# Attention scores of two heads: a zero-padded 128-row matmul, or two 64-row matmuls on separate halves of the array

## The chip, the cores and the metric

The kernel runs on one core of a Trainium2 chip. The metric is the device time of one execution in microseconds (us), from launch to end; smaller is better. A profile of one execution shows what each engine did: PE is the matrix engine (PEld are its weight loads, which the profile lists apart), DVE the vector engine, ACT the scalar engine, POOL the general one, SP the queue that issues most of the DMAs. In a matmul the first operand is *stationary* (it is loaded into the array ahead of time) and the second *moving* (it streams through, one column after the other); the result goes to PSUM, which has eight banks of 512 f32 columns per partition.

## The reference, cut to what matters

A four-layer decoder trunk with 256 tokens, model width 1024 and head width 64. Layers 0 and 3 use differential attention, layer 1 block-sparse attention (with 256 tokens it is plain causal attention), layer 2 grouped attention with a window of 128, a bias and sinks. Each layer is followed by a squared-ReLU MLP. What the change touches is the product of queries and keys, which in every layer is made for 16 head maps of width 64:

```python
# differential: H = 8 heads, each with two maps c (q and k are 64 wide)
s = jnp.einsum('bqhcd,bkhcd->bhcqk', qi, k)
s = jnp.where(causal, s, -inf); p = softmax(s)
p = p[:, :, 0] - lam * p[:, :, 1]
# block-sparse and windowed layers: 16 heads of width 64
s = einsum('...qd,...kd->...qk', q, k)
```

## The kernel before, in words

All products are done on f32 values split into a high and a low part. A value x is copied to the type f32r (the high part), and x minus that copy is the low part. A product then takes three matmuls: high by high, high by low, low by high (`mm3`, L269 to L273). Where the high and low parts of the moving operand lie side by side, two instructions do (`block_step`, L571 to L573).

Weights come in pieces of 1 MB by DMA (`fetch`). `stage` splits each piece with four ACT copies (L79, tile `whi`) and four DVE subtractions (L80, tile `wlo`); `take` keeps this two pieces ahead of the matmuls. The instructions are emitted in the order of the Python code, and a list scheduler then orders each engine's queue; semaphores are placed by it. It may move independent matmuls of a projection (`p_in`) in between those of the attention.

A mixer layer (`mixer_layer`) makes its projections one after the other. In layers 0, 1 and 3 the order is v, pair 0, pair 1, v, pair 2, pair 3, where a *pair* c brings the queries and keys of four heads (two *blocks* of two heads). Layer 2 has one key block for all, and four pieces of queries. While one projection runs, the blocks of the pair before it are worked off: the first in the middle of it (`midway`), the second after it. So there are 8 blocks in a layer and 32 in all. After the last projection nothing of the kind is left to run beside the last two blocks except the output projection (`out_proj`, tile `p_d`), which needs the blocks' results one after the other.

A block goes through `turn` (queries and keys are transposed by PE into a PSUM bank, tile `p_qk`), `put_q` (L467 and L468, tile `qhl`), `put_k` (L471 to L475, keys into the tiles `kpadh` and `kpadl`), `scores` (L311), the softmax (L331 on DVE, L334 on ACT), a transposition (`p_t`, L349), the product with v (`p_av`), and a transposition back (`p_o`, L374) into `oo`.

The two heads of a block lie on partitions 0 to 63 and 64 to 127 of one transposed query tile. So that one matmul over all 128 rows gives the scores of both heads side by side, the keys are stored padded: `kpad` has a place for each head of the two, and the 64 partitions of the other head hold zeros there. `new_keys` (L359) makes the zeros with eight POOL memsets (L365) at each layer, and `put_k` writes only the 64 partitions that belong to the head, in one ACT copy and one DVE subtraction for each head:

```python
for h in range(2):
    s = slice(HD * h, HD * h + HD)
    A.activation(k[0][s, :n, h, :], p[s], AF.Copy)
    V.tensor_tensor(k[1][s, :n, h, :], p[s], f(k[0][s, :n, h, :]), op=OP.subtract)
```

A block's scores are then six matmuls with 128 rows: for the first 128 tokens three with 2 x 128 = 256 moving columns into bank `p_s0`, for the other 128 tokens three with 2 x 256 = 512 columns into bank `p_s1` (both are called `p_s` in the profile).

Of the kernel before, what the change touches and what calls it, by code (L numbers as in the profile page):

```python
# [24 lines left out]
HD = 64  # L25
# [9 lines left out]
def f(ap):  # L35
    return ap.bitcast(F32)
# [3 lines left out]
def trunk(ctx: ExitStack, tc: tile.TileContext, xT, positions, gains, lams, swa_row, fng, weights, out):  # L40
    nc = tc.nc
    V, A, G, T = nc.vector, nc.scalar, nc.gpsimd, nc.tensor
# [226 lines left out]
    def mm3(out, lh, ll, rh, rl, start, stop, **kw):  # L269

        T.matmul(out, lh, rh, start=start, stop=False, **kw)  # L271
        T.matmul(out, lh, rl, start=False, stop=False, **kw)  # L272
        T.matmul(out, ll, rh, start=False, stop=stop, **kw)  # L273
# [37 lines left out]
    def scores(q, k, mask, sinks):  # L311


        p0, p1 = bank("wk", "p_s0"), bank("wk", "p_s1")
        (qh, ql), (kh, kl) = q, k
        for p, t, n in ((p0, 0, P), (p1, 1, S)):
            o = p[:, :2 * n].rearrange("p (h m) -> p h m", h=2)
            a = slice(P * t, P * t + P)
            mm3(o, qh[:, a], ql[:, a], kh[:, :, :n], kl[:, :, :n], True, True)
        out = []  # L320
        scored[0] += 1
        pair_e = room(4 + scored[0] % 2, [P, 2, 3 * P], "e")
        for c in range(2):
            ns = sb.tile([P, 3 * P], F32, tag="ns", name="ns", bufs=2)
            nm = tiny.tile([P, NT], F32, tag="nm", name="nm", bufs=4)
            l = tiny.tile([P, NT], F32, tag="l", name="l", bufs=6)
            e = pair_e[:, c]
            mk = mask[:, :, :].rearrange("p a b -> p (a b)")
            for t, p, n in ((0, p0, P), (1, p1, S)):
                s = slice(0, P) if t == 0 else slice(P, 3 * P)  # L330
                V.tensor_tensor_reduce(ns[:, s], p[:, n * c:n * c + n], mk[:, s], op0=OP.add, op1=OP.min,  # L331
                                       scale=-1.0, scalar=3.0e38 if sinks is None else sinks[c][1],
                                       accum_out=nm[:, t:t + 1])
# [24 lines left out]

    def new_keys():  # L359

        kpad = [[room(10 + 2 * j + x, [P, 2, 2, S], f"kpad{'hl'[x]}{j}", F32R) for x in range(2)] for j in range(2)]
        for j in range(2):
            for x in range(2):
                for h in range(2):
                    G.memset(f(kpad[j][x][HD * (1 - h):HD * (1 - h) + HD, :, h, :]), 0.0)  # L365
        return kpad

    pair = []

# [82 lines left out]
    def turn(src, n):  # L452

        p = bank("wk", "p_qk")
        for b in range(n):
            for t in range(NT):
                at = S * b + P * t
                T.transpose(p[:, at:at + P], src(b, t), ident)
        return p[:, :S * n].rearrange("p (b m) -> p b m", m=S)
# [9 lines left out]
        return q  # L469

    def put_k(k, p, n):  # L471
        for h in range(2):
            s = slice(HD * h, HD * h + HD)
            A.activation(k[0][s, :n, h, :], p[s], AF.Copy)
            V.tensor_tensor(k[1][s, :n, h, :], p[s], f(k[0][s, :n, h, :]), op=OP.subtract)  # L475

    def mixer_layer(i, n):
        mixer, slot = i % 3, i // 3
        r = norm_factor(n)
        parts = []  # L480
        kpad = new_keys()
        if mixer == 2:
            bias = room(8, [P, 1024], "bias")
            rest = room(9, [P, 1024], "rest")
# [4 lines left out]
            p = proj(n, (256, 1), True)  # L489
            kv = rest[:, 512:1024].rearrange("p (t c) -> p t c", t=NT)  # L490
            for t in range(NT):
                V.scalar_tensor_tensor(kv[:, t, :], p[t], r[:, t:t + 1], rest[:, :256],
                                       op0=OP.mult, op1=OP.add)
            rope(kv[:, :, 0:P].rearrange("p t (s e) -> p t s e", e=HD), 2)
            put_k(kpad[0], turn(lambda b, t: kv[:, t, 0:P], 1), 1)
            kT = [x[:, 0] for x in kpad[0]]
            first, second = [], []
            for c in range(4):
                p = proj(n, (256, 1), False, first)
                qn = room(c % 2, [P, NT, 256], "qn")  # L500
                for t in range(NT):
                    for h in range(2):
                        s = slice(P * h, P * h + P)
                        o = qn[:, t, :].rearrange("p (b h e) -> p b h e", h=2, e=HD)[:, :, h, :]
# [6 lines left out]
                qs = []  # L511
# [12 lines left out]
        else:  # L524
            v = [room(8 + j, [P, NT, 512], f"v{j}") for j in range(2)]
            vdone = 0
            first, second = [], []
            for c in ("v", 0, 1, "v", 2, 3):
                p = proj(n, (512, 2), vdone == 0, first)
                if i == 0 and used[0] == 2:  # L530
                    rotary_tables()
                    lambdas()
                if c == "v":
                    for t in range(NT):
                        A.activation(v[vdone][:, t, :], p[t], AF.Copy, scale=r[:, t:t + 1])
# [12 lines left out]

                def block(b, c=c, qs=qs, qk=qk):
                    if b == 0:  # L550
                        qs += put_q(turn(lambda j, t: qk[:, t, P * j:P * j + P], 2))
                        put_k(kpad[c % 2], turn(lambda j, t: qk[:, t, P * (2 + j):P * (2 + j) + P], 2), 2)
                    q, k = [x[:, b] for x in qs], [x[:, b] for x in kpad[c % 2]]
                    h = 2 * c + b
                    vh = lambda m: v[h // 4][:, m, P * (h % 4):P * (h % 4) + P]
                    if mixer == 0:
                        step(diff_block(parts, slot, q, k, vh, h))
                    else:
                        step(head_block(parts, q, k, vh, causal, None, h))

                first, second = [lambda f=block: f(0)], [lambda f=block: f(1)]
# [228 lines left out]
```

## Time and profile before

| | |
|---|---|
| median of three runs | 1183.45 us (1182.74 to 1184.18) |
| the profiled execution | 1184.6 us, of which its instructions span 1182.8 us |
| mean granted clock of TensorE | 0.994 |
| PE, PEld, DVE, ACT, POOL busy | 1154.8, 993.3, 860.0, 705.9, 19.7 us |

How to read the rows. In the groups, a row is: line, engine, operation, written tile <- read tiles, shape written <- shape read, times it ran | busy us in all, mean ns of one | idle us of the engine just before them and what ended that idle time. In the timeline, a row is: start in us, duration in us, engine, line, operation and tiles, and, in brackets, the idle time before it and what ended it; x8 means that eight of them are merged into the row. In the stages, a row is: start:end, length, busy us of each engine with its instructions, granted clock, DMA share and GB/s. The end of a matmul is modelled: its duration holds time in which the next is already streaming, so what matmuls cost in a row is read from the distance of their starts.

### The profile page before, as it was taken

Reading aid. Unit: us, or ns where it says so; the run is one execution under the profiler, and the core shown is the slowest. Engines: PE = TensorE matmul, PEld = TensorE weight load, DVE = VectorE, ACT = ScalarE, POOL = GpSimd, SP = SyncE. Lnnn points to the kernel's source line nnn. Section 1 sums busy time; section 2 is a strip of 40 time slices with the busy share of each in tenths; the row PEclk is TensorE's granted clock in tenths of the full one; section 3 lists DMA queues with packets and bytes.
Section 4 is the critical chain, followed back from the end, with each engine's and each line's share of the span. In section 5 each row is a group of like instructions: output and inputs, shape, how many; then the busy total and the mean of one; then the engine's idle time right before and its main releaser. Section 6 shows DMA issues by size and latency. Waiting matters only on the chain.

```text
span 1182.8 us, 17907 instructions
## 1 busy us (share of the span) xinstructions
PE 1154.8 (98%) x6448; PEld 993.3 (84%) x6448; DVE 860.0 (73%) x2190; ACT 705.9 (60%) x1619; POOL 19.7 (2%) x55
## 2 busy tenths in 40 slices
PE   9997999999999999999999999999999989999996
PEld 7885888888888888888899988888888868888885
DVE  6989988656665698775668798775557798777453
ACT  7786766555466775554547775654447776566341
POOL 2000000000100000000010000000010000000000
PEclk9999999999999999999999999999999999999999
DMA  8532455555544255555563245555654433555541
GB/s 323 199 132 104 143 201 191 182 209 179 180 160 157 73 178 178 184 208 178 183 224 111 75 153 206 190 202 178 201 189 144 143 107 108 186 182 178 188 174 37
DMA packets 30122, 198.74 MB, mean 168 GB/s; under 512 B 3536, under 2 KB 4688, under 8 KB 6608
## 3 DMA queue, kind: packets, MB, share of 16 engines
q1 hardware_dynamic: 29744, 197.06, 48.4%
q8 instruction: 51, 0.84, 0.3%
q10 hardware_dynamic: 288, 0.52, 0.1%
q14 instruction: 39, 0.32, 0.1%
HBM read 196.52 MB, written 1.05 MB: 167 GB/s over the span
## 4 chain that ended last, share of the span: by engine, by line
PE 93%; DVE 4%; ACT 2%; DMA 0%; issue 0%; SPq 0%
PE p_up L572 20%; PE p_down L572 15%; PE p_up L573 10%; PE p_down L573 8%; PE p_in L272 6%; PE p_in L273 6%; PE p_in L271 6%; PE p_e L572 3%; PE p_d L572 2%; PE p_last L273 2%; PE p_last L272 2%; PE p_last L271 2%; PE p_t L349 1%; PE p_e L573 1%; DVE wlo L80 1%; PE p_d L573 1%
## 5 line engine op out<-in xcount | busy, mean ns | idle before, releaser
L80 DVE TENSOR_TENSOR wlo<-raw,whi 128x512 fp32r<-128x512 f32 x740 | 484.2, 685 | 239.9 <-ACT whi L79 239.3
L79 ACT ACTIVATE whi<-raw 128x512 fp32r<-128x512 f32 x740 | 419.9, 623 | 295.2 <-PE p_up L572 106.7
L572 PE MATMUL p_up<-hg,whi 128*128 128x512 f32 x1024 | 358.3, 395 | 0.0
L573 PE MATMUL p_up<-hg,wlo 128*128 128x256 f32 x1024 | 285.2, 279 | 0.0
L572 PE MATMUL p_down<-uu,whi 128*128 128x512 f32 x768 | 266.4, 393 | 0.0
L572 PEld LDWEIGHTS p_up<-hg,whi 128*128 128x128 f32 x1024 | 192.0, 188 | 44.5 <-DVE hg L229 0.2
L573 PE MATMUL p_down<-uu,wlo 128*128 128x256 f32 x768 | 213.5, 278 | 0.0
L573 PEld LDWEIGHTS p_up<-hg,wlo 128*128 128x128 f32 x1024 | 192.9, 188 | 0.2
L572 PEld LDWEIGHTS p_down<-uu,whi 128*128 128x128 f32 x768 | 143.9, 187 | 32.8
L573 PEld LDWEIGHTS p_down<-uu,wlo 128*128 128x128 f32 x768 | 144.5, 188 | 0.0
L271 PE MATMUL p_in<-whi,hg 128*128 128x512 f32 (+1 forms) x368 | 137.1, 374 | 0.1
L272 PE MATMUL p_in<-wlo,hg 128*128 128x512 f32 (+1 forms) x368 | 136.0, 370 | 0.2 <-DVE wlo L80 0.2
L273 PE MATMUL p_in<-whi,hg 128*128 128x512 f32 (+1 forms) x368 | 135.6, 368 | 0.0
L272 PEld LDWEIGHTS p_in<-wlo,hg 128*128 128x128 f32 x368 | 69.6, 189 | 12.4 <-DVE wlo L80 1.5
L271 PEld LDWEIGHTS p_in<-whi,hg 128*128 128x128 f32 x368 | 69.5, 189 | 11.6 <-ACT whi L79 0.7
L273 PEld LDWEIGHTS p_in<-whi,hg 128*128 128x128 f32 x368 | 69.5, 189 | 10.7
L578 ACT ACTIVATE cross<-p_up 128x256 f32<-128x256 f32 x128 | 48.1, 376 | 31.2 <-ACT whi L79 22.3
L334 ACT ACTIVATE e<-ns,nm 128x256 f32<-128x256 f32 (+1 forms) x128 | 56.7, 446 | 14.4 <-DVE nm L331 14.0
L572 PE MATMUL p_d<-oo,whi 128*128 128x512 f32 x128 | 50.9, 428 | 10.2 <-DVE oo L384 10.2
L579 DVE TENSOR_TENSOR relu<-p_up,cross 128x256 f32<-128x256 f32 x128 | 53.2, 417 | 0.3
L271 PE MATMUL p_last<-whi,uu 128*128 128x512 f32 x128 | 49.8, 389 | 0.0
L273 PE MATMUL p_last<-whi,uu 128*128 128x512 f32 x128 | 49.8, 389 | 0.0
(182 smaller groups left out, 1368.9 us busy)
## 6 DMA issues: line engine op xcount, KB each, us to landing
raw<-in_weights SPq DMA_DIRECT2D x183, 1024.0 KB, 4.9
raw<-in_weights SPq DMA_DIRECT2D x8, 256.0 KB, 5.7
hT<-in_xT SPq DMA_DIRECT2D x4, 256.0 KB, 5.8
bias<-in_swa_row SPq DMA_DIRECT2D x1, 512.0 KB, 5.2
grow<-in_fng SPq DMA_DIRECT2D x1, 512.0 KB, 3.7
out<-res ACTq DMA_DIRECT2D x2, 256.0 KB, 2.8
out<-res SPq DMA_DIRECT2D x2, 256.0 KB, 2.7
lv<-in_lams SPq DMA_DIRECT2D x1, 256.0 KB, 6.4
```

The source lines that it names most:

```text
L79: A.activation(hi[:, s], raw[:, s], AF.Copy)
L80: V.tensor_tensor(lo[:, s], raw[:, s], f(hi[:, s]), op=OP.subtract)
L271: T.matmul(out, lh, rh, start=start, stop=False, **kw)
L272: T.matmul(out, lh, rl, start=False, stop=False, **kw)
L273: T.matmul(out, ll, rh, start=False, stop=stop, **kw)
L334: A.activation(e[:, s], ns[:, s], AF.Exp, bias=nm[:, t:t + 1], scale=-1.0, accum_out=l[:, t:t + 1])
L349: T.transpose(p[:, P * j:P * j + P], e[:, P * j:P * j + P], ident)
L572: T.matmul(r3(2)(p), hi, x, start=start, stop=False, skip_group_check=True)
L573: T.matmul(p[:, :S], lo, x[:, 0], start=False, stop=stop, skip_group_check=True)
L578: A.activation(cross, p[:, S:], AF.Copy)
L579: V.tensor_tensor(out, p[:, :S], cross, op=OP.add)
```

## The change

The keys are no longer padded. A tile `kk` holds for a pair the high and low part of both blocks' keys, with head 0 on partitions 0 to 63 and head 1 on partitions 64 to 127, as the transposition left them. `new_keys` no longer sets zeros, and `put_k` is one ACT copy and one DVE subtraction over 128 partitions.

`scores` now issues, for each of the two token halves and each of the three products, one matmul for each head: rows 0 to 63 for head 0, rows 64 to 127 for head 1, each into a bank of its own (`ps_h[0]`, `ps_h[1]`). That is 12 matmuls with 64 rows instead of six with 128, with 128 and 256 moving columns instead of 256 and 512. A head's bank holds both token halves, so the softmax's reads (L331) of a head come from one bank instead of two.

```diff
-        p0, p1 = bank("wk", "p_s0"), bank("wk", "p_s1")
+        ps_h = [bank("wk", f"p_s{c}") for c in range(2)]
         (qh, ql), (kh, kl) = q, k
-        for p, t, n in ((p0, 0, P), (p1, 1, S)):
-            o = p[:, :2 * n].rearrange("p (h m) -> p h m", h=2)
+        for cols, t, n in ((slice(0, P), 0, P), (slice(P, 3 * P), 1, S)):
             a = slice(P * t, P * t + P)
-            mm3(o, qh[:, a], ql[:, a], kh[:, :, :n], kl[:, :, :n], True, True)
+            for x, y, first, last in ((qh, kh, True, False), (qh, kl, False, False), (ql, kh, False, True)):
+                for c in range(2):
+                    r = slice(HD * c, HD * c + HD)
+                    T.matmul(ps_h[c][:, cols], x[r, a], y[r, :n], start=first, stop=last)
...
-            for t, p, n in ((0, p0, P), (1, p1, S)):
+            for t in range(NT):
                 s = slice(0, P) if t == 0 else slice(P, 3 * P)
-                V.tensor_tensor_reduce(ns[:, s], p[:, n * c:n * c + n], mk[:, s], op0=OP.add, op1=OP.min,
+                V.tensor_tensor_reduce(ns[:, s], ps_h[c][:, s], mk[:, s], op0=OP.add, op1=OP.min,
...
     def new_keys():
-        kpad = [[room(10 + 2 * j + x, [P, 2, 2, S], f"kpad{'hl'[x]}{j}", F32R) for x in range(2)] for j in range(2)]
-        for j in range(2):
-            for x in range(2):
-                for h in range(2):
-                    G.memset(f(kpad[j][x][HD * (1 - h):HD * (1 - h) + HD, :, h, :]), 0.0)
-        return kpad
+        return [room(10 + j, [P, 2, 2, S], f"kk{j}", F32R) for j in range(2)]
...
     def put_k(k, p, n):
-        for h in range(2):
-            s = slice(HD * h, HD * h + HD)
-            A.activation(k[0][s, :n, h, :], p[s], AF.Copy)
-            V.tensor_tensor(k[1][s, :n, h, :], p[s], f(k[0][s, :n, h, :]), op=OP.subtract)
+        A.activation(k[:, 0, :n], p, AF.Copy)
+        V.tensor_tensor(k[:, 1, :n], p, f(k[:, 0, :n]), op=OP.subtract)
...
-                    q, k = [x[:, b] for x in qs], [x[:, b] for x in kpad[c % 2]]
+                    q, k = [x[:, b] for x in qs], [kk[c % 2][:, x, b] for x in range(2)]
```

More of the change, by code (lines that the diff above doesn't have):

```diff
@@ L480, in mixer_layer @@
         parts = []
-        kpad = new_keys()
+        kk = new_keys()
         if mixer == 2:
@@ L494, in mixer_layer @@
             rope(kv[:, :, 0:P].rearrange("p t (s e) -> p t s e", e=HD), 2)
-            put_k(kpad[0], turn(lambda b, t: kv[:, t, 0:P], 1), 1)
-            kT = [x[:, 0] for x in kpad[0]]
+            put_k(kk[0], turn(lambda b, t: kv[:, t, 0:P], 1), 1)
+            kT = [kk[0][:, x, 0] for x in range(2)]
             first, second = [], []
@@ L551, in block @@
                         qs += put_q(turn(lambda j, t: qk[:, t, P * j:P * j + P], 2))
-                        put_k(kpad[c % 2], turn(lambda j, t: qk[:, t, P * (2 + j):P * (2 + j) + P], 2), 2)
-                    q, k = [x[:, b] for x in qs], [x[:, b] for x in kpad[c % 2]]
+                        put_k(kk[c % 2], turn(lambda j, t: qk[:, t, P * (2 + j):P * (2 + j) + P], 2), 2)
+                    q, k = [x[:, b] for x in qs], [kk[c % 2][:, x, b] for x in range(2)]
                     h = 2 * c + b
```

## The prediction

> **What bounds the kernel now.** I read the page first, for the busy shares and the chain that ended last.
>
> ```profile
> PE 1154.8 (98%) x6448; PEld 993.3 (84%) x6448; DVE 860.0 (73%) x2190; ACT 705.9 (60%) x1619; POOL 19.7 (2%) x55
> ...
> PE 93%; DVE 4%; ACT 2%; DMA 0%; issue 0%; SPq 0%
> ```
>
> PE holds 93% of the chain. So a change to its work counts almost in full, and work taken from DVE, ACT or POOL counts only where PE waits for it. There are as many weight loads as matmuls (6448 each): every matmul brings its own load. Second, the stages, to see where PE does wait:
>
> ```profile
> 14.00:92.00 78.00, 77.69 (x388) 63.35 (x387) 68.81 (x262) 61.85 (x153) 0.00 (x0) 1.00 0.58 212
> 92.00:119.00 27.00, 18.69 (x109) 14.46 (x108) 23.48 (x124) 16.55 (x58) 0.00 (x0) 1.00 0.22 79
> ...
> 948.00:980.00 32.00, 25.54 (x131) 20.14 (x129) 27.70 (x151) 20.22 (x70) 0.00 (x0) 0.84 0.29 99
> ```
>
> While projections run (14 to 92 us here) PE is busy without a hole. In the last two blocks of layers 0 and 3 (92 to 119, 948 to 980) it is not: there PE idles 8.3 and 6.5 us, and the chain of each block through DVE and ACT sets the pace. I call these four blocks the tails; the other 28 run under a full PE. Third, the groups of the scores, each shape by itself:
>
> ```profile
> L271 PE MATMUL p_s<-kpadh,qhl 128*128 128x512 f32 x32 | 13.7, 428 | 0.0
> ...
> L273 PE MATMUL p_s<-kpadh,qhl 128*128 128x256 f32 x32 | 9.1, 284 | 0.0
> ```
>
> First and last of six such rows, one for each product and shape: 32 blocks of six matmuls. Their durations overlap, so fourth, the timeline of one block under a full PE, for the distance of their starts:
>
> ```profile
> 53.28 0.28 PE L273 MATMUL p_s<-kpadh,qhl 128*128 128x256 f32 x1
> 53.28 0.19 PEld L271 LDWEIGHTS p_s<-kpadh,qhl 128*128 128x128 f32 x1
> ...
> 53.40 0.39 PE L271 MATMUL p_s<-kpadh,qhl 128*128 128x512 f32 x1
> 53.40 0.19 PEld L272 LDWEIGHTS p_s<-kpadl,qhl 128*128 128x128 f32 x1
> 53.63 0.40 PE L272 MATMUL p_s<-kpadl,qhl 128*128 128x512 f32 x1
> ...
> 54.09 1.03 PE L458 MATMUL p_qk<-ident,qk 128*128 128x128 f32 x8
> ```
>
> A matmul with 256 columns costs 53.40 - 53.28 = 0.12 us, one with 512 costs 53.63 - 53.40 = 0.23. The load of a matmul starts when the matmul before it starts, so it is hidden. A block costs 3 x 0.12 + 3 x 0.23 = 1.05 us, all 32 cost 34 us: that is all there is to win here, 3% of the span, and half of it is the most that two heads side by side can give.
>
> **The matmuls.** After the change each head has its own: 6 with 128 columns and 6 with 256. The nearest row for 128 columns is the last one above, eight transpositions of 128 x 128: (1.03 - 0.27) / 7 = 0.11 us each, where 0.27 is the duration of one of them. They are not of this type, but each also needs a load, and the loads above follow each other at 0.12; so I take 0.11.
>
> If the two heads' matmuls run side by side, loads included, a pair costs what one costs: 3 x 0.11 + 3 x 0.12 = 0.69 us, 0.36 less than now. If they take turns, all 12 count: 6 x 0.11 + 6 x 0.12 = 1.38, which is 0.33 more. No matmul in this trace uses less than 128 rows, so both ends stand. I take the first: adjacent matmuls of the new code differ in rows, stationary operand and bank, so they share nothing that the code shows. For the 28 blocks under a full PE that is 28 x 0.36 = 10.1 us less.
>
> The Trainium skill, "TensorE: Matmul & The Clock Gate", part "Packing small matmuls", says of matmuls on different row groups that they run concurrently, with starts some 4 ns apart; by that rule a block is at 0.69. No run here shows it yet, and the section "LDWEIGHTS" adds that a load's time goes by its columns and not its rows, so that 64-row loads would be no cheaper; if they also queue, a block is at 1.38.
>
> **The switch of shape.** The array goes from 128 rows to 64 at each block and back: 64 switches. Their price is not in this trace. The lower end is nothing: around the block above PE goes over to transpositions (54.09) after two steps of 0.23 after 53.63, with one more score between and no gap. The upper end is a pipeline that has to run empty with the load behind it. A matmul's duration goes beyond its share by 0.28 - 0.12 = 0.16, and what a load costs when it is not hidden is in the tail of layer 0:
>
> ```profile
> 95.32 0.38 PE L349 MATMUL p_t<-ident,e 128*128 128x128 f32 x2
> 96.90 0.62 PE L271 MATMUL p_s<-kpadh,qhl 128*128 128x256 f32 x2 [1.20 <-ACT kpadh L474]
> 97.63 0.39 PE L272 MATMUL p_s<-kpadl,qhl 128*128 128x256 f32 x1
> 97.85 0.28 PE L273 MATMUL p_s<-kpadh,qhl 128*128 128x256 f32 x1
> 97.97 0.40 PE L272 MATMUL p_s<-kpadl,qhl 128*128 128x512 f32 x1
> ```
>
> The matmul at 97.63 has waited for its operand, so its load is bare: the next starts 0.22 later, where the next pair is 0.12 apart. A bare load costs 0.10 to 0.11. So a switch costs 0 to 0.16 + 0.11 = 0.27 us. I take 0.11, a bare load, between the ends and the nearest thing that PE shows when its flow is broken: 64 x 0.11 = 7.0 us more.
>
> **The keys.** `put_k` runs 13 times, and in each one ACT copy and one DVE subtraction go, while the others grow from 64 to 128 partitions. Growing costs nothing: `put_q`'s copy on 128 partitions takes the 587 ns of `put_k`'s on 64.
>
> ```profile
> L475 DVE TENSOR_TENSOR kpadl<-p_qk,kpadh 64x512 fp32r<-64x512 f32 x24 | 16.4, 684 | 5.7 <-ACT kpadh L474 5.6
> ...
> L474 ACT ACTIVATE kpadh<-p_qk 64x512 fp32r<-64x512 f32 x24 | 14.1, 587 | 3.7 <-DVE kpadl L475 3.5
> ...
> L467 ACT ACTIVATE qhl<-p_qk 128x512 fp32r<-128x512 f32 x16 | 9.4, 587 | 3.1 <-PE p_qk L458 3.1
> ```
>
> DVE and ACT are relieved of about half of 16.4 and 14.1 us, POOL of most of the 19.7 us it is busy in all. Under a full PE this is worth nothing: at 14 to 92 us DVE has 9 us to spare, and if the six blocks there make that stretch 2.2 us shorter, DVE's own work shrinks by three subtractions, 2.1 us. The cover holds.
>
> In the tail it counts. The row of L474 names an order that the code does not ask for: ACT's copy for head 1 waits for DVE's subtraction for head 0. In time:
>
> ```profile
> 93.12 0.58 ACT L474 ACTIVATE kpadh<-p_qk 64x512 fp32r<-64x512 f32 x1
> ...
> 96.25 0.59 ACT L474 ACTIVATE kpadh<-p_qk 64x512 fp32r<-64x512 f32 x1
> 95.19 0.67 DVE L475 TENSOR_TENSOR kpadl<-p_qk,kpadh 64x512 fp32r<-64x512 f32 x1
> ...
> 96.88 0.69 DVE L475 TENSOR_TENSOR kpadl<-p_qk,kpadh 64x512 fp32r<-64x512 f32 x1 [0.20 <-ACT kpadh L474]
> 956.80 0.60 ACT kpadh L474
> ```
>
> The first score starts at 96.90 (the fence above), when the second copy ends. After the change the high keys are whole at 93.7 and the low ones, with DVE's queue unchanged, at 95.9. The transpositions ahead of the scores on PE (95.32, two of them at 0.11) leave it at about 95.5, so the scores start 1.4 us earlier, and their second part at 95.9 instead of 97.63. The last row, from the chain of waits, has the same step in layer 3. What comes next is DVE's softmax, which in the tails is 87% busy (23.48 of 27), so the gain may shrink to nothing; I take 1.4 for each tail, 2.8 us less.
>
> **The later read.** A head's bank now holds both token halves. If the order is kept by bank, the first read of head 0 waits for 11 of 12 matmuls instead of three of six.
>
> ```profile
> 102.67 0.36 PE L271 MATMUL p_s<-kpadh,qhl 128*128 128x256 f32 x1
> 103.31 0.29 DVE L331 CUSTOM_DVE_ANT_0 ns<-p_s,causal 128x128 f32<-128x128 f32 x1
> ...
> 104.65 0.42 DVE L331 CUSTOM_DVE_ANT_0 ns<-p_s,causal 128x256 f32<-128x256 f32 x1
> ```
>
> Now the last read starts 1.98 us after the first score. With pairs all scores have streamed after 0.69 and ended 0.28 later; three reads, by these rows' durations 0.29 + 0.42 + 0.29, bring the last to 1.97: no change. Taking turns, it is 0.69 later, in four tail blocks 2.8 us. Under a full PE the read that waits holds up what is queued behind it on DVE, the subtractions of `stage` (L80); these run two pieces of weights ahead of the matmuls that need them, and a few tenths of a microsecond in a block do not use that lead up. I count nothing.
>
> **The sum.** -10.1 (matmuls) + 7.0 (switches) - 2.8 (keys) = -5.9 us. Against the profiled execution's 1184.6 (a span of 1182.8 and 1.8 around it) that is 1178.7. That execution lies 1.15 above the median of the runs, so in their terms 1177.5. With the switch at its ends the case spans 12.9 less to 4.4 more: 1170.5 to 1188.
>
> **Rivals.** *The heads take turns* (slower). The loads are the mechanism: in the timeline under a full PE the loads at 53.28 and 53.40 lie 0.12 apart, each starting only with the matmul before it. If a 64-row load needs the same path as a 128-row one, 12 loads set the block at 1.38 us whatever the matmuls do. Price: 32 x 0.33 = 10.6, plus 2.8 for late reads, minus 2.8 for the keys, plus 0 to 7.0 for switches: 1194 to 1201. It decides as soon as a pair costs more than 0.175 us on average, 1.05 / 6. For it speaks that all loads shown come one after the other; against it only that the two heads' rows are not shared.
>
> *The switch costs the whole emptying* (slower). Pairs work, but each of 64 switches costs 0.27, and where a pair's first block waits for its low keys between its scores, as at 97.63, the scheduler may fill the break with projections, which adds two switches in 16 blocks, 32 more. 96 x 0.27 = 25.9, minus 12.9: 13 more, 1196.5. From 12.9 / 96 = 0.13 us a switch, the change loses. Against it: the transpositions go in and out with no gap. The Trainium skill's "TensorEngine Tiling (Array Packing)", "Key Properties", says that a change of tiling mode drains the engine; that is this rival's mechanism, and no row of this case can bear it out, as all matmuls here are 128*128.
>
> *Both together*: 10.6 for turns and 64 x 0.27 = 17.3 for switches, 1211.
>
> *The change does not do what it says*: matmuls with 128 columns do not get cheaper than those with 256 by more than the load allows, or even stream at half rate, 0.22. Then pairs cost 3 x 0.22 + 3 x 0.12 = 1.02 us, the matmuls give nothing, and the sum is +4: 1187.
>
> **Chances.** Pairs with a modest switch 0.41; turns 0.27; the full switch 0.17; both 0.10; half rate 0.05. The forecast is the first, 1177.5. From 1168 (its lower end with more won in the tails) to 1201 the range leaves out the combined rival and little else. A change of 0.2%, 2.4 us, is about what a measurement can tell from none. Within the first case a switch above 0.165 us would end the gain, so of its 0.41 some 0.36 fall below that, and 0.04 come from a full switch that is not quite full: faster 0.40. Same 0.08. The rest, slower, 0.52: the likeliest single case is a gain, the cases that lose hold together slightly more.
>
> **What would show it.** Right: `p_s` matmuls in pairs whose starts lie a few hundredths apart, a pair each 0.11 to 0.12 us; a distance from the last projection matmul to the first score, and back, near 0.11 above the usual; `put_k` with 13 copies near 0.59 and the first tail's scores near 95.5. Wrong: 12 starts at 0.11 to 0.12 (turns), holes of 0.2 to 0.3 us on both sides of each block (drain), or a tail whose scores start no earlier.

## The result, and the profile after

The kernel after takes 1191.18 us (median of four runs, 1190.4 to 1191.41), the kernel before beside it 1183.33 (1182.74 to 1184.18). The ratio is 1.0067, 95% interval 1.0052 to 1.0082: 7.85 us slower, where 5.9 us faster was forecast. The profiled execution took 1191.38 us, its instructions 1189.6.

The page of after, first the busy shares, then the chain that ended last:

```profile
PE 1161.6 (98%) x6640; PEld 994.2 (84%) x6640; DVE 853.4 (72%) x2177; ACT 699.5 (59%) x1606; POOL 3.1 (0%) x23
...
PE 89%; DVE 6%; ACT 4%; issue 1%; DMA 0%; SPq 0%
```

DVE, ACT and POOL are relieved as foreseen (by 6.6, 6.4 and 16.6 us), and PE, the engine that counts, is busy for 6.8 us longer, with 192 more instructions. Where in the span? The stages of after, one row for the mixer of each layer, from the first `p_in` to the first `p_up` (start:end, length, then busy us of PE, PEld, DVE, ACT and POOL, granted clock, DMA share, GB/s):

```profile
6.06:133.63 127.57, 119.64 (x636) 94.62 (x637) 109.20 (x418) 93.32 (x242) 0.00 (x0) 0.99 0.49 177
311.78:433.97 122.19, 121.62 (x710) 102.03 (x709) 78.77 (x229) 78.11 (x191) 0.00 (x0) 1.00 0.39 136
612.12:696.98 84.86, 83.87 (x649) 76.16 (x648) 67.21 (x237) 56.45 (x164) 0.00 (x0) 1.00 0.32 110
875.05:1000.77 125.72, 117.86 (x639) 95.15 (x637) 97.20 (x364) 83.08 (x223) 0.00 (x0) 0.99 0.38 132
```

The same four rows of before:

```profile
5.70:130.71 125.01, 116.08 (x589) 93.72 (x589) 110.40 (x422) 95.41 (x246) 2.34 (x13) 1.00 0.50 181
308.64:429.32 120.68, 120.68 (x663) 101.88 (x661) 82.24 (x233) 80.01 (x195) 1.20 (x3) 1.00 0.40 138
607.46:689.47 82.01, 81.49 (x600) 75.97 (x599) 67.51 (x238) 56.88 (x165) 1.14 (x3) 1.00 0.33 115
867.63:993.86 126.23, 118.05 (x590) 96.69 (x589) 98.61 (x368) 85.12 (x227) 1.13 (x3) 0.96 0.38 131
```

Layers 1 and 2 are longer by 1.51 and 2.85 us, with a granted clock of 1.00 in all four rows. Layer 0 is 2.56 longer and layer 3 looks 0.5 shorter, but there the clock differs: 0.99 against 1.00, and 0.99 against 0.96. It is lower only at the *end* of these two layers, from the last projection matmul to the first `p_up` (three blocks and the output projection). The ends of layers 0 and 3 in before, then in after, and then the end of layer 0 in headorder, a kernel with after's matmuls in another order (below):

```profile
86.49:130.71 44.22, 35.73 (x210) 28.99 (x209) 40.61 (x180) 32.04 (x98) 0.00 (x0) 1.00 0.28 96
947.01:993.86 46.85, 39.30 (x210) 32.18 (x209) 40.77 (x180) 32.15 (x98) 0.00 (x0) 0.89 0.26 90
88.61:133.63 45.02, 38.06 (x228) 30.56 (x227) 40.11 (x170) 31.35 (x95) 0.00 (x0) 0.96 0.28 94
955.64:1000.77 45.13, 38.05 (x229) 30.66 (x227) 40.16 (x170) 31.32 (x95) 0.00 (x0) 0.96 0.28 93
89.50:132.95 43.45, 36.55 (x229) 29.40 (x227) 39.95 (x170) 31.58 (x95) 0.00 (x0) 1.00 0.29 97
```

The two ends of one kernel are the same work: headorder's second, at 1.00 too, also takes 43.45. Before's second, at 0.89, takes 2.6 us more than its first at 1.00. In after 3.41 us of each end ran at half the clock (0.50 from 108.95 to 112.36 and from 975.94 to 979.35). By before's two ends that costs 0.9 us; in keyorder, whose ends have 0.96 and 1.00, it is 1.2. So after's ends at the full clock would take 43.8 to 44.2 us, an estimate from these rows, against before's 44.22: they lose nothing. What is lost lies ahead of them, at 1.00 in both kernels: up to the last projection matmul layer 0 takes 82.55 us instead of 80.79 and layer 3 80.59 instead of 79.38, which is 1.76 and 1.21 more. The MLP stages between the mixers keep their lengths to a few tenths. So every mixer layer loses, by 1.2 to 2.9 us, and where projections run beside the blocks.

The groups of after, the scores and the keys:

```profile
L322 PE MATMUL p_s<-kk,qhl 64*128 64x128 f32 x192 | 26.4, 299 | 1.1 <-ACT et L353 0.4 <-DVE o L433 0.3 <-DVE qhl L466 0.3
L322 PE MATMUL p_s<-kk,qhl 64*128 64x256 f32 x192 | 20.7, 295 | 0.0
...
L471 DVE TENSOR_TENSOR kk<-p_qk,kk 128x512 fp32r<-128x512 f32 x12 | 8.2, 681 | 0.0
...
L470 ACT ACTIVATE kk<-p_qk 128x512 fp32r<-128x512 f32 x12 | 7.1, 593 | 0.0
```

The work is as the prediction counted it: 384 matmuls with 64 rows, and key copies that do not grow dearer on 128 partitions (593 and 681 ns beside 587 and 684 before). What the groups do not show is what stands between the matmuls. That is in the timeline of the first block of after (start, duration, engine; x2 and x10 are merged rows):

```profile
44.57 0.39 PE L272 MATMUL p_in<-wlo,hg 128*128 128x512 f32 x1
...
44.88 0.19 PEld L322 LDWEIGHTS p_s<-kk,qhl 64*128 64x128 f32 x2 [0.36 <-ACT kk L470]
44.89 0.33 PE L322 MATMUL p_s<-kk,qhl 64*128 64x128 f32 x2
45.14 0.19 PEld L273 LDWEIGHTS p_in<-whi,hg 128*128 128x128 f32 x1
45.15 0.50 PE L273 MATMUL p_in<-whi,hg 128*128 128x512 f32 x1
45.25 0.19 PEld L271 LDWEIGHTS p_in<-whi,hg 128*128 128x128 f32 x1
...
45.48 0.40 PE L271 MATMUL p_in<-whi,hg 128*128 128x512 f32 x1
...
45.80 0.64 PEld L322 LDWEIGHTS p_s<-kk,qhl 64*128 64x128 f32 x10 [0.36 <-DVE kk L471]
45.80 0.84 PE L322 MATMUL p_s<-kk,qhl 64*128 64x128 f32 x10
...
46.58 0.19 PEld L272 LDWEIGHTS p_in<-wlo,hg 128*128 128x128 f32 x1
46.58 0.50 PE L272 MATMUL p_in<-wlo,hg 128*128 128x512 f32 x1
46.69 0.19 PEld L273 LDWEIGHTS p_in<-whi,hg 128*128 128x128 f32 x1
...
46.92 0.40 PE L273 MATMUL p_in<-whi,hg 128*128 128x512 f32 x1
```

Three things are to be read here. **The pairs are pairs:** the two matmuls of the x2 row start 3 ns apart in the unrounded records, and so do their loads (4 ns); the ten matmuls of the second run need 46.58 - 45.80 = 0.78 us, change of shape included, where ten starts in turn at 0.11 to 0.12 would need 1.15. **The switch:** the load with 64 rows does not start with the matmul ahead of it at 44.57, as loads here do between equal shapes, but at 44.88, which is 0.08 after that matmul's 0.23 are over. (The rows name the copies of the keys as what was waited for, but these had ended 0.17 and 0.25 us before the two loads, at 44.71 and 45.55; behind the matmul ahead both loads come 0.08 to 0.09 late, and so does the one in sw64 below, which needs no key.) On the way back the next projection's load starts at 45.14 and is bare: from the projection at 45.15 to the one at 45.48 there are 0.33 instead of 0.23. From 44.57 to 45.48 the usual distances would be 0.23 + 0.11 + 0.23; measured are 0.91, so 0.34 us go into there and back. For the second run (45.48 to 46.92) it is 1.44 less 0.23 + 0.57 + 0.23, or 0.41. **The count:** this block is not one run of 12 matmuls but two, of 2 and 10, because the low keys were not ready; 0.6 us of projection was put in between, and the shape changed twice more.

I went through the whole trace of after in this way: each unbroken run of 64-row matmuls, the time from the start of the matmul ahead of it to the start of the second matmul behind it, less the usual distances (0.23, 0.12 or 0.11 for the 128-row ones by their columns, 0.11 or 0.12 for each pair). There are **54 runs**, so 108 switches where 64 were assumed: ten blocks are whole, the other 22 are broken in two (mostly 1 + 11 or 2 + 10). The median of what a run costs beyond its matmuls is **0.40 us**; the sum is 27.5, in which some runs hold waits as well. Where a later text says "runs" and "extra", this count is meant.

Part by part, 0.40 for each run less 0.36 for each block:

| part (blocks) | runs | 0.40 x runs - 0.36 x blocks | measured |
|---|---|---|---|
| layer 0, up to its last projection (5) | 10 | +2.2 | +1.76 |
| layer 1 (8) | 11 | +1.5 | +1.51 |
| layer 2 (8) | 11 | +1.5 | +2.85 |
| layer 3, up to its last projection (5) | 10 | +2.2 | +1.21 |
| the ends of layers 0 and 3 (6) | 12 | +2.6 | -0.1 to -1.5 at the full clock |
| sum | 54 | +10.0 | +5.8 to +7.2; median of the executions +7.85 |

For the ends the measured bounds are the estimate above (-0.1 to -0.7 for both) and headorder's 43.45 twice (-1.5).

In layer 2 four of the 11 runs hold 0.94 to 1.08 beyond their matmuls. In two of these that I followed, the matmuls stop for about half a microsecond in mid-run, in a stretch where the waits of the loads name `qhl`, `et` and `o`. I have not separated that further.

### The profile page after: what moved, and what is told of

The parts are those of the page before. It is cut to its first block, busy times and chain, and to the rows that moved or that the text cites. A ratio compares the mean times of both kernels' runs of the same rounds, so it can differ in the third digit from the quotient of the medians.

```text
span 1189.6 us, 18171 instructions
## 1 busy us (share of the span) xinstructions
PE 1161.6 (98%) x6640; PEld 994.2 (84%) x6640; DVE 853.4 (72%) x2177; ACT 699.5 (59%) x1606; POOL 3.1 (0%) x23
## 4 chain that ended last, share of the span: by engine, by line
PE 89%; DVE 6%; ACT 4%; issue 1%; DMA 0%; SPq 0%
PE p_up L568 20%; PE p_down L568 15%; PE p_up L569 10%; PE p_down L569 8%; PE p_in L272 6%; PE p_in L271 6%; PE p_in L273 6%; PE p_e L568 3%; PE p_last L273 2%; PE p_last L271 2%; PE p_last L272 2%; PE p_d L568 2%; PE p_s L322 2%; DVE wlo L80 2%; PE p_e L569 1%; ACT whi L79 1%
## 5 line engine op out<-in xcount | busy, mean ns | idle before, releaser
L271 PEld LDWEIGHTS p_in<-whi,hg 128*128 128x128 f32 x368 | 69.5, 189 | 12.7 <-ACT whi L79 1.2
L337 ACT ACTIVATE e<-ns,nm 128x128 f32<-128x128 f32 (+1 forms) x128 | 56.9, 446 | 14.7 <-DVE nm L334 14.6
L271 PE MATMUL p_last<-whi,uu 128*128 128x512 f32 x128 | 49.8, 389 | 0.0
L272 PE MATMUL p_last<-wlo,uu 128*128 128x512 f32 x128 | 49.8, 389 | 0.0
```

## The experiments

Each ratio is to the kernel before, timed on the same chip, with its 95% interval.

**sw64** and **sw128**: the switch by itself, where nothing else changes. In the kernel before, behind each of the 64 groups of up-projection matmuls, go two 64-row matmuls on separate halves with 256 columns (sw64), or one with 128 rows in the same place (sw128). Nobody reads what they write.

```diff
+            for c in range(2):                                  # sw64
+                x = bank("acc", f"p_x{c}")
+                T.matmul(x[:, :S], hi[HD * c:HD * c + HD, 7, P:], n.both[3][HD * c:HD * c + HD, 1, 0], start=True, stop=True)
```
```diff
+            x = bank("acc", "p_x")                              # sw128
+            T.matmul(x[:, :S], hi[:, 7, P:], n.both[3][:, 1, 0], start=True, stop=True)
```

> The kernel before with one pair of 64-row matmuls (64 x 128 weights, 256 moving columns, one on each half of the rows, into two banks that nobody reads) added after each of the 64 groups of up-projection matmuls, where PE has no holes. Theory (the switch of rows is what costs): the pair streams in about 0.12 us, but going to 64 rows and back costs 0.33 to 0.41 us more, as around the runs of 64-row matmuls in the changed kernel: 64 x 0.48 = 31 us slower than before, 1214. Rival (the switch is cheap, the changed kernel lost its time to waits for keys and banks): 64 x 0.12 = 7.7 us, 1191, the same as with one 128-row matmul in that place.

> The same place and number, but one matmul with 128 rows and 256 moving columns instead of the pair. Both theories: 64 x 0.12 = 7.7 us slower than before, 1191. It is the yardstick: the pair's kernel minus this one is 64 switches there and back.

Measured: sw64 1224.67 us, 1.0352 (1.0335 to 1.0370); sw128 1198.50, 1.0125 (1.0099 to 1.0151). The difference is 26.2 us, or **0.41 us for there and back, 0.20 for a switch**; the up stages of the two profiled executions, 16 insertions each, differ by 6.1 to 6.6 us, which is 0.38 to 0.41 each. That is the tighter measure, as one of the four executions of sw128 took 1193.25 us, some 5 less than the others. The timeline of sw64 around one insertion:

```profile
136.86 0.28 PE L573 MATMUL p_up<-hg,wlo 128*128 128x256 f32 x1
...
137.06 0.19 PEld L624 LDWEIGHTS p_x<-hg,whi 64*128 64x128 f32 x2 [0.25 <-PE p_up L573]
137.07 0.39 PE L624 MATMUL p_x<-hg,whi 64*128 64x256 f32 x2
137.38 0.19 PEld L572 LDWEIGHTS p_up<-hg,whi 128*128 128x128 f32 x1
137.38 0.50 PE L572 MATMUL p_up<-hg,whi 128*128 128x512 f32 x1
...
137.72 0.28 PE L573 MATMUL p_up<-hg,wlo 128*128 128x256 f32 x1
```

and the same place in sw128:

```profile
137.21 0.28 PE L573 MATMUL p_up<-hg,wlo 128*128 128x256 f32 x1
137.22 0.19 PEld L623 LDWEIGHTS p_x<-hg,whi 128*128 128x128 f32 x1
...
137.33 0.28 PE L623 MATMUL p_x<-hg,whi 128*128 128x256 f32 x1
...
137.45 0.40 PE L572 MATMUL p_up<-hg,whi 128*128 128x512 f32 x1
...
137.69 0.28 PE L573 MATMUL p_up<-hg,wlo 128*128 128x256 f32 x1
```

From `p_up` through the insertion to the second `p_up` behind it sw128 takes 0.48 us, sw64 0.86. In sw128 the load starts with the matmul ahead of it (137.21, 137.22). In sw64 it starts 0.20 behind it, 0.08 to 0.09 after that matmul's 0.12 are over. From there to the next start, 137.07 to 137.38, are 0.31: the pair's 0.12, 0.08 to 0.09 for an emptying again, and 0.11 that are left. From 137.38 to 137.72 are 0.34 where 0.23 are usual, and again 0.11 are left. That is what a bare load cost in before (0.10 to 0.11), and I read it so: a switch is an emptying of about 0.09 and a bare load of 0.11. One thing is open: sw128 as a whole costs 0.24 an insertion, not the 0.12 that the rows show. The 512-column steps around it, in the down stages too, go at 236 ns instead of 231; what slows them is not known. They do so in sw64 too, so the difference is free of it.

**sw64one**: as sw64, with one of the two matmuls.

```diff
-            for c in range(2):
-                x = bank("acc", f"p_x{c}")
-                T.matmul(x[:, :S], hi[HD * c:HD * c + HD, 7, P:], n.both[3][HD * c:HD * c + HD, 1, 0], start=True, stop=True)
+            x = bank("acc", "p_x")
+            T.matmul(x[:, :S], hi[:HD, 7, P:], n.both[3][:HD, 1, 0], start=True, stop=True)
```

> As the kernel with the added pair of 64-row matmuls in the up-projection (1224.7), but head 0's half alone: one matmul on rows 0 to 63. Theory (the switch there and back costs 0.40 us for the run, and the second of a pair is free): within 2 us of the kernel with the pair, 1223 to 1225. Rival (each 64-row load or matmul is dear by itself, and the pair paid for two): 64 x 0.1 to 0.2 = 6 to 13 us less, 1212 to 1218.

Measured: 1224.49 us, 1.0346 (1.0328 to 1.0364), the same as the pair. The second matmul of a pair is free; what costs is the run.

**headorder**: the three products of head 0, then those of head 1, in each half of tokens. If pairs depended on adjacent matmuls of different halves, this would take them away.

```diff
-            for x, y, first, last in ((qh, kh, True, False), (qh, kl, False, False), (ql, kh, False, True)):
-                for c in range(2):
+            for c in range(2):
+                for x, y, first, last in ((qh, kh, True, False), (qh, kl, False, False), (ql, kh, False, True)):
```

> The changed kernel with the loop over heads outside that over the three products: head 0's three matmuls, then head 1's, for each token half. Theory (pairs run side by side only where the two heads' matmuls are neighbours in the queue, because PE starts them in order): a block's 12 matmuls go from 0.69 back towards 1.38 us, 32 x 0.6 = about 19 us slower than the changed kernel, 1210. Rival (the array works on both halves whatever the order, or pairs never were worth anything): 1191 as the changed kernel.

Measured: 1192.99 us, 1.0084 (1.0069 to 1.0099), 1.8 above after, and the intervals overlap. The first theory fell. In the queue of this kernel the heads do stand in threes, apart from the first matmuls of some broken blocks, and in the trace the halves still run side by side, most starts 3 to 11 ns apart: the sequence in which they are issued hardly matters.

**samehalf**: both heads' matmuls read rows 0 to 63, so none can run beside another; head 1's own scores are left out.

```diff
-                    r = slice(HD * c, HD * c + HD)
+                    r = slice(0, HD)
```

> The changed kernel with both heads' score matmuls on rows 0 to 63, so that no two of the 12 can share the array. Left out: head 1's scores (it gets those of head 0). Number and size of matmuls, loads, switches, banks and reads stay. Theory (a block's 12 matmuls cost 0.69 us because the halves work side by side): 32 x 0.69 = 22 us slower than the changed kernel, 1213; less where PE waits in the tails. Rival (the pairs' starts lie close only on paper, and the time goes by the switch alone): 1191 as the changed kernel.

Measured: 1201.22 us, 1.0141 (1.0121 to 1.0162), 10.0 above after. The timeline around the same run of ten as above:

```profile
45.72 0.40 PE L271 MATMUL p_in<-whi,hg 128*128 128x512 f32 x1
...
46.05 1.42 PE L322 MATMUL p_s<-kk,qhl 64*128 64x128 f32 x10
...
47.40 0.19 PEld L272 LDWEIGHTS p_in<-wlo,hg 128*128 128x128 f32 x1
```

Ten in turn need 1.35 from the first start to the way back, against 0.78 in pairs; that is what turns look like, and after does not have them. The number of runs is the same 54, their extra 43.8 instead of 27.5, so 16.3 us more PE time. The time rose by 10.0 only, because it did not rise everywhere. Layers 1 and 2 are 4.3 and 6.3 us longer than in after (about 1 of the 6.3 goes with a granted clock of 0.98), layers 0 and 3 up to their last projection 2.6 and 2.5; PE got 4.7, 3.6, 2.9 and 2.5 us more work there. So beside projections PE time counts nearly one for one. At the ends of layers 0 and 3 PE got 1.3 us more in each, and they take 43.10 us at the full clock, no more than headorder's 43.45: there the work went into PE's waits.

**full128**: no 64-row matmul, no switch and no pair: the padded keys of before, twelve matmuls a block with 128 rows, one head each, into the banks of after.

```diff
+            for x, y, first, last in ((qh, kh, True, False), (qh, kl, False, False), (ql, kh, False, True)):
+                for c in range(2):
+                    T.matmul(ps_h[c][:, cols], x[:, a], y[:, c, :n], start=first, stop=last)
```

> The kernel before (padded keys, two steps for each head) with the changed kernel's 12 matmuls, banks and reads, but each matmul with all 128 rows, the other head's being zeros. So there is neither a switch nor a pair. Theory: 12 loads and matmuls in turn, 1.38 instead of 1.05 us a block, 32 x 0.33 = 10.6 us slower than before, and up to 3 for the later reads in the tails: 1194 to 1197. Rival (bank layout and held order cost much by themselves): over 1200.

Measured: 1199.86 us, 1.0143 (1.0128 to 1.0158). Twelve in turn are 32 x 0.33 = 10.6 by the prediction's working; 16.7 were measured. The other 6 us were not taken apart in full; the one other thing that this edit changes is the bank of a head's scores, and with it the later reads. PE waits 3.0 us for `et` ahead of the score matmuls of full128, 0.9 in before and 1.0 in after, which has the same banks: so that wait, at least, is not what after loses its time to.

**keyorder**: before, with both copies of a pair's keys issued ahead of both subtractions.

```diff
             A.activation(k[0][s, :n, h, :], p[s], AF.Copy)
+        for h in range(2):
+            s = slice(HD * h, HD * h + HD)
             V.tensor_tensor(k[1][s, :n, h, :], p[s], f(k[0][s, :n, h, :]), op=OP.subtract)
```

> The kernel before with only the order in the key step changed: both heads' high copies first, then both subtractions, so that ACT's second copy does not wait for DVE's first subtraction. Theory (the key step counts only in the tails of layers 0 and 3): 1 to 1.5 us in each, 2 to 3 us faster than before, 1180.5. Rival (DVE sets the pace there and gives the gain back): 1183, within 1 us of before.

Measured: 1182.21 us, 0.9993 (0.9985 to 1.0002): no change. The last projection and the first tail scores of layer 0 in keyorder's timeline:

```profile
87.23 0.39 PE L273 MATMUL p_in<-whi,hg 128*128 128x512 f32 x1
...
96.05 0.60 PE L271 MATMUL p_s<-kpadh,qhl 128*128 128x256 f32 x2
97.83 0.39 PE L272 MATMUL p_s<-kpadl,qhl 128*128 128x256 f32 x1 [0.96 <-DVE kpadl L477]
```

and the end of its layer 3, which ran at the full clock (that of layer 0 did not: 44.59 us at 0.96):

```profile
948.41:991.80 43.39, 35.74 (x210) 29.27 (x209) 40.20 (x177) 32.11 (x97) 0.00 (x0) 1.00 0.29 96
```

From the last projection the first tail score starts after 8.82 us instead of 10.41 (before's were at 86.49 and 96.90), 1.6 earlier. At the full clock the end takes 43.39 us instead of before's 44.22, so half of that arrives. The kernel as a whole gains nothing, because what lies ahead of the ends got longer: up to the last projection layer 0 takes 81.56 us (80.79 in before) and layer 3 79.78 (79.38). Why that is so was not followed.

**scoresonly**: after, with the keys again in two copies and two subtractions.

```diff
+        for h in range(2):
+            s = slice(HD * h, HD * h + HD)
+            A.activation(k[s, 0, :n], p[s], AF.Copy)
+            V.tensor_tensor(k[s, 1, :n], p[s], f(k[s, 0, :n]), op=OP.subtract)
```

> The changed kernel with the key step in two halves again, one copy and one subtraction for each head on 64 partitions (no zeros needed). Theory: what the matmuls' change alone costs; the key step's gain is gone (2 to 3 us), and the program has 59 instead of 54 runs of 64-row matmuls, 5 x 0.37 = 2 us: 1195. Rival (the key step is worth nothing): 1191 to 1193.

Measured: 1197.82 us, 1.0125 (1.0111 to 1.0138), 6.6 slower than after. There are 59 runs with an extra of 34.3. So the undivided keys are worth 6.6 us, but for the most part in a place where the prediction did not look, under a full PE (layer 1 alone, at the full clock in both, is 124.73 us instead of 122.19): with half of the keys late, blocks fall into more pieces, with longer waits between.

**lowfirst**: after, with the product that needs the low keys first, so that a block starts only when all its operands are there.

```diff
-            for x, y, first, last in ((qh, kh, True, False), (qh, kl, False, False), (ql, kh, False, True)):
+            for x, y, first, last in ((qh, kl, True, False), (ql, kh, False, False), (qh, kh, False, True)):
```

> The changed kernel with the three products in another order: query high by key low, query low by key high, and high by high last. So the first score waits for the low keys, and the scheduler has no cause to break a block's 12 matmuls in two at the wait for them: 46 runs of 64-row matmuls instead of 54. Theory (each run costs about 0.37 us beside its matmuls): 8 x 0.37 = 3 us faster than the changed kernel, 1188. Rival (waits, not switches): unchanged or slower, 1191 to 1193, as the scores start later.

Measured: 1195.05 us, 1.0105 (1.0091 to 1.0119), slower than after. Runs fell from 54 to 46 only, because 14 blocks are still broken, 13 of them by transpositions of the block ahead (`p_t`) that stand between; and in the tails the scores now start later, 11.08 us behind the last projection of layer 0 instead of 9.50. Part of the loss is the clock: the ends of layers 0 and 3 had 0.93 in the profiled execution, after's 0.96. Layer 1, at the full clock in both and with one run less, is 0.4 shorter (121.77 against 122.19).

**merged**: the scores of a pair's two blocks in one go, low keys first: runs of 24 matmuls.

```diff
+        if not made:
+            made.extend(score_mms(*qk) for qk in zip(q, k))
+        ps_h = made.pop(0)
```

> As the one before, and the scores of both blocks of a pair are issued together, 24 matmuls in one go, so that there are 17 runs of 64-row matmuls instead of 54. Theory: 37 x 0.37 = 13.7 us faster than the changed kernel, 1177.5, and 6 faster than the one before the change, if the two PSUM banks that are held longer cost nothing. Rival (switches are not it): 1191 or slower, since banks are short.

Measured: 1185.99 us, 1.0022 (1.0010 to 1.0034), 5.2 better than after with 17 runs. It shows the switch's share by its removal. In layer 1, at the full clock in both, seven runs less than in after make 2.73 us (119.46 against 122.19), 0.39 each, and the layer is now shorter than in before (120.68):

```profile
312.18:431.64 119.46, 118.85 (x710) 101.25 (x709) 78.75 (x229) 77.26 (x191) 0.00 (x0) 1.00 0.41 139
```

Four runs there, each saving 2 x 0.36 for 0.40, are 1.28 less; 1.22 are measured. The forecast, 13.7 better than after, missed in layers 0 and 3. Two runs in each have 2.0 to 2.5 us extra, waits included, and the granted clock is lower at their ends, 0.89 and 0.88 where after has 0.96. The end of layer 0:

```profile
89.15:134.04 44.89, 37.08 (x216) 31.07 (x215) 38.20 (x161) 30.27 (x91) 0.00 (x0) 0.89 0.27 95
```

Of merged's twelve executions the one with a mean clock of 0.996, like after's 0.995 to 0.997, took 1182.05 us, and the three with 0.986 took 1188.27 to 1188.63. So about 4 of the 8.5 us that are missing go with the clock. Why less of it was granted here was not followed.

**hybrid**: merged for the first three pairs of a layer; the two blocks of the last pair, the tail, one by one with the high keys first (the cut below is against merged).

```diff
-                    q = [[x[:, j] for x in qs] for j in range(2)]
+                    js = range(2) if c < 3 else [b]
+                    q = [[x[:, j] for x in qs] for j in js]
```

> The kernel with both blocks' scores in one go, but only for the first three pairs of a layer; the last pair's two blocks are scored one by one, high by high first, as in the changed kernel, since in the tails of layers 0 and 3 the 24 matmuls in one go held back what PE has to do for the blocks before (p_o waited 1.1 and 1.5 us behind them). 29 runs of 64-row matmuls instead of 54 and 17. Theory (0.4 us for each run, plus waits in the tails): 25 x 0.4 = 10 us faster than the changed kernel, 1181, a little faster than before the change. Rival (the banks held longer cost as much under a full PE as in the tails): 1186 as the kernel with all pairs in one go.

Measured: 1180.46 us (1179.72 to 1181.41), 0.9973 (0.9964 to 0.9982), faster than both kernels, with 29 runs, and that at a lower granted clock (0.991 to 0.994; the median of before's executions beside it is 0.995).

**hybrid2**: hybrid in layers 0, 1 and 3; layer 2 with the padded keys and 128-row scores of before.

```diff
+        score = scores if sinks is None else padded_scores
...
-        es, ls = zip(*scores(q, k, mask, sinks))
+        es, ls = zip(*score(q, k, mask, sinks))
```

> hybrid in layers 0, 1 and 3; layer 2, the one without key differences where hybrid's attention part took 83.51 us against 82.01 before, goes back to the padded 128-row scores. Theory (a switch there and back costs about 0.40 us, and layer 2 lost by its switches alone): layer 2 returns to about 82.0, the rest stays, 1180.46 - 1.5 = 1179.0. Rival (layer 2's loss lies in its neighbours or is chance): 1180.5, no change against hybrid.

Measured: 1178.95 us (1178.58 to 1180.09), 0.9963 (0.9949 to 0.9977). Its mixer of layers 1, 2 and 3:

```profile
309.73:428.64 118.91, 118.83 (x711) 101.36 (x709) 78.60 (x229) 77.30 (x191) 0.00 (x0) 1.00 0.41 140
606.78:689.24 82.46, 81.92 (x601) 76.01 (x600) 67.61 (x238) 56.89 (x165) 0.00 (x0) 1.00 0.33 115
867.31:988.14 120.83, 113.88 (x639) 94.15 (x638) 96.63 (x364) 82.83 (x223) 0.00 (x0) 0.99 0.40 137
```

Layer 2 went from 83.50 to 82.46, 1.0 of the 1.5 foreseen; layer 3 was 1.0 shorter in this execution too, with nothing changed there: in hybrid 3.41 us ahead of its last projection ran at a clock of 0.50 (943.14 to 946.55), in hybrid2 none did. The interval overlaps hybrid's, so the last step is likely but not settled. What is settled is that a kernel with 64-row pairs beats before by 3 to 5 us, once a layer has 6 to 8 runs instead of 11 to 16. Whether padded keys in the same grouping and order would gain as much was not run.

## Why the prediction was wrong, point by point

**What bounds the kernel.** PE does, as read, and the division of the blocks held: in samehalf PE time counted nearly one for one beside the projections and not at all at the ends of layers 0 and 3, which hold one block more each than its tails. What the reading passed over is the clock. Its row for 948 to 980 us shows 0.84, and a lower clock at the ends makes single stages and whole executions differ by 1 to 6 us (merged's twelve range from 1182.05 to 1188.63). It does not turn the sign here: the stages that lose are at 1.00.

**The matmuls, -10.1.** Right. Pairs start 3 ns apart, loads too, and cost 0.11 and 0.12; at 0.36 a block all 32 save 11.5. The rule quoted from the Trainium skill, "TensorE: Matmul & The Clock Gate", part "Packing small matmuls" (concurrent, starts some 4 ns apart), agrees with the trace. The loads do not queue, and so "The heads take turns" fell: samehalf shows what turns would have cost. Half rate for 128 columns fell with it.

**The switch, +7.0: this step failed.** It was put at 64 x 0.11. Measured are 54 runs at 0.40, 21.6 us: three times as much. Both factors were off, and in the prediction's own sum either error alone (64 x 0.20 or 108 x 0.11) would have left about no change; both together turn the sign.
- The price, 0.20 instead of 0.11. The prediction had the right upper end, "a pipeline that has to run empty with the load behind it", 0.16 + 0.11, and took the load alone, since "the transpositions go in and out with no gap". That row was no likeness: transpositions have 128 rows like everything else in before, so nothing in them changes shape, and they say nothing about a change of shape. The emptying is there, 0.09 of the 0.16, and the load behind it is bare, 0.11.
- The count, 108 instead of 64. That a block can be split where it waits for its low keys was written down, but in the rival only, with 16 blocks; 22 of 32 are split, also around the transpositions of the block ahead.

The rival "The switch costs the whole emptying" was right in kind: 96 switches at 0.27 were expected there, 108 at 0.20 were found, and its own turning point, 0.13 us, lies below what was measured. The Trainium skill's "TensorEngine Tiling (Array Packing)", "Key Properties", says that a change of tiling mode drains the engine; in the trace the 64-row load starts 0.31 us after the matmul ahead of it (44.57 to 44.88) instead of with it. The chance of 0.17 for this rival was too low: the only evidence against it was the row that could not speak on it. All chances together had slower at 0.52; the time that was named was the likeliest single case, at 0.41.

**The keys, -2.8.** The step held, and about half of its worth arrived. Copies stay at 593 ns, but the first tail score of after comes 9.50 us behind the last projection instead of 10.41, 0.9 earlier and not 1.4. At the full clock the end of a layer is 0.8 us shorter with earlier keys (43.45 in headorder and 43.39 in keyorder, 44.22 in before), or 1.5 to 1.7 of the 2.8 for the two tails. "The gain may shrink to nothing" was written; the value taken was the other end. Most of what the keys are worth in after, 6.6 us, lies elsewhere: they keep runs whole and the waits between pieces short (scoresonly).

**The later read, 0.** Here it was not nothing on DVE. The reads of the first half of tokens in after:

```profile
L334 DVE CUSTOM_DVE_ANT_0 ns<-p_s,causal 128x128 f32<-128x128 f32 x48 | 13.7, 286 | 8.6 <-PE p_s L322 8.6
...
L334 DVE CUSTOM_DVE_ANT_0 ns<-p_s,band,rest 128x128 f32<-128x128 f32 x16 | 5.5, 346 | 4.1 <-PE p_s L322 4.1
```

They wait 12.7 us; in before all reads of scores together wait 7.6. How much of these 5 us lies on the path is not known. DVE's share of the chain rose from 4 to 6%, and this may be part of it.

**The sum again.** In layers 1 and 2, and in layers 0 and 3 up to their last projections, are 26 blocks and 42 runs: -9.4 + 16.8 = +7.4 us, where 7.3 were measured, in layer 2 more than its share and in layer 3 less. At the ends of layers 0 and 3 the six blocks and 12 runs would add 2.6 us, but there PE's waits and the earlier keys leave -0.1 to -1.5 at the full clock. Together that is 5.8 to 7.2 us of the 7.85, whose interval is 6.2 to 9.7.

## What to carry to other kernels

Matmuls that use half of the array's rows do run two at a time, loads included, but the way there and back costs 0.40 us here: before packing, count how many unbroken runs the scheduler will leave, not how many matmuls are saved. A run must save more than one there and back (here 12 matmuls do not, 24 do), so gather them, and make operands arrive whole before a run starts, except where another engine is waiting for its first result. A price that the trace before cannot show should not be taken from a row in which the thing does not happen. And stages of two kernels are to be compared only where their granted clocks agree: here 0.96 instead of 1.00 over 45 us was worth about 1 us, as much as the effects in question.

## What the runs showed of the hardware that was not expected

- A change between 128-row and 64-row matmuls and back costs 0.41 us (26.2 us / 64; 0.38 to 0.41 in single stages), and it costs the same whether one or two half-height matmuls stand between (1224.49 and 1224.67 us).
- Two loads on separate halves start together (4 ns apart), just as the matmuls do; and head by head in place of pair by pair makes 1.8 us in 384 matmuls (intervals overlap), so partners need not be neighbours in the queue.
- Taken in turn, a 64-row matmul of 128 or 256 columns is no cheaper than one with 128 rows: in samehalf ten take 1.35 us with a switch of 0.20 in it, 0.115 each, where with 128 rows 0.11 to 0.12 were measured.
- At the ends of layers 0 and 3 the clock was granted at half for 3.41 us in the profiled execution of after (0.50 from 108.95 to 112.36) and not at all in that of headorder (1.00): the same end of before took 44.22 us at a mean of 1.00 and 46.85 at 0.89.
